# Low parts of the down-projection weights: an adding DMA in place of a VectorE subtraction

## The chip, the cores and the metric

The kernel runs on one core of a Trainium2 chip. The core has TensorE (matrix products, PE in the profile), VectorE (DVE), ScalarE (ACT), GpSimd (POOL) and SyncE (SP, which issues nearly all DMAs), an on-chip memory of 128 partitions (SBUF), accumulators for TensorE (PSUM) and 16 DMA engines. The metric is the device time of one execution in microseconds (us), the median of several runs.

## The reference

One layer of a streaming encoder, in float32, for a group of 512 tokens and a group of 8 x 16 tokens, which share all weights (640 tokens in all, D = 1024):

```python
x = x + 0.5 * swiglu(rms_norm(x, p['norm_ffn1']), p['w_ffn1_up'], p['w_ffn1_down'])
m, st = mixer(rms_norm(x, p['norm_mix']), p, lb, cache, win_rows)
x = x + m
x = x + 0.5 * swiglu(rms_norm(x, p['norm_ffn2']), p['w_ffn2_up'], p['w_ffn2_down'])

def swiglu(h, w_up, w_down):
    gate, val = jnp.split(h @ w_up, 2, axis=-1)
    return (jax.nn.silu(gate) * val) @ w_down
```

The mixer holds a windowed attention, a gated linear recurrence and a convolution with a scan; the change does not touch it. It touches the last product of each SwiGLU, the down-projection: `w_down` has 2816 rows and 1024 columns.

## The kernel before, in words

Activations stand transposed, with features on the partitions and the 640 tokens along a row, in two halves of 320. TensorE multiplies in fp32r, a rounded form of float32. To keep float32's accuracy each operand is split in a high part (the value rounded to fp32r) and a low part (the value minus the high part), and a product is the sum of three: high x high, high x low, low x high.

An item of `proj` is one 128-column strip of a weight matrix with `nk` blocks of 128 rows. Its weight is loaded into a buffer `wr` (three of them), rounded into `wh` (two of them) by ScalarE or VectorE, and the difference goes into `wl` (two of them) by a VectorE subtraction. Then TensorE runs six matmuls for each block: two halves of `wh` with the activations' high parts, two of `wh` with their low parts, two of `wl` with their high parts, into two accumulators `pp`. An item with 8 blocks has 48 matmuls, one with 6 blocks 36.

A feed-forward part (`ffn`) runs in three stages over rows of the hidden size: rows 0 to 5 (in blocks of 128), 6 to 13 and 14 to 21. In the first stage the hidden values come from plain `proj` items with 8 blocks each, in the others from `pair`, which computes seven products of combinations instead of eight, and whose own splits (lines 799 to 829) run on VectorE and ScalarE and use one `wl`, one `wh` and one `wr` as well. At the end of each stage stand eight down-projection items, `proj(wd, ...)` (line 879), one per block of output columns, whose result VectorE adds to the residual (L373). So there are 2 x 3 stages with 8 down-projection items each: 16 items with 6 blocks and 32 with 8. The third stage of the first part also stores the residual and prepares the next norm, that of the second part writes the output.

The order of the work is made before the program is built: `Sched` plays all operations through with costs (a VectorE pass 0.066 us + 1.042 ns an element, a DMA by its bytes) and gives each engine its list; an engine works its list strictly in that order and waits at each instruction for what it needs. `lag` sets how many items ahead an operation is due: 4 for a weight load, 2 for the rounding, 1.5 for the subtraction. A buffer is given to the next item when its last reader is through: `wr` after the rounding and the subtraction, `wl` after the item's last matmul.

Of the kernel before, what the change touches and what calls it, by code (L numbers as in the profile page):

```python
# [8 lines left out]
F32 = mybir.dt.float32  # L9
# [3 lines left out]
AF = mybir.ActivationFunctionType  # L13
ALU = mybir.AluOpType
AX = mybir.AxisListType

P = 128
# [28 lines left out]
class View:  # L46
# [14 lines left out]
    def r(self, pattern, **sizes):  # L61
        return self._then(lambda a: a.rearrange(pattern, **sizes))
# [273 lines left out]
def trunk_kernel(ctx: ExitStack, tc: tile.TileContext, A: dict, O: list):  # L336
    nc = tc.nc
    S = Sched()
# [7 lines left out]
    def dve(n, f, aps=0):  # L346
        return ("DVE", 0.066 + 1.042e-3 * n + 0.063 * aps, f)

    def act(n, f, aps=0, src=None):
        return ("ACT", 0.1 + 0.833e-3 * n + 0.093 * aps - (0.049 if src is not None and src.in_psum else 0.0), f)  # L350
# [7 lines left out]
    def tt(out, a, b, op, only=None):  # L358
        alts = [dve(out.n, lambda: nc.vector.tensor_tensor(out(), a(), b(), op=op))]  # L359
        return S.op(pick(alts, only), [a, b], [out])  # L360
# [11 lines left out]
    def stt(out, a, s, b, op0, op1):  # L372
        return S.op([dve(out.n, lambda: nc.vector.scalar_tensor_tensor(out(), a(), ap_of(s), b(), op0=op0, op1=op1),  # L373
                         isinstance(s, View))], [a, s, b], [out])

    def fn(out, a, func, scale=1.0, bias=0.0, accum=None):
        aps = isinstance(scale, View) + isinstance(bias, View) + (accum is not None)
        kw = {}

        def f():  # L380
            if accum is not None:
                kw["accum_out"] = accum()
            nc.scalar.activation(out(), a(), func, bias=ap_of(bias), scale=ap_of(scale), **kw)  # L383

        return S.op([act(out.n, f, aps, a)], [a, scale, bias], [out] + ([accum] if accum is not None else []),
                    func=None if func in ANY_TABLE else func)
# [15 lines left out]
    def dma(out, a, lag=None):  # L402
        v = out if isinstance(out, View) else a
        return S.op([("SP", 0.47, lambda: nc.sync.dma_start(ap_of(out), ap_of(a)))], [a], [out],  # L404
                    dma=v.n * 4 * v.proto.shape[0], lag=lag)

    def mm(calls):

        def cost(o, l, m):
            if l.proto.dtype == F32R:  # L410
                return max(0.144, m.n * 0.4583e-3)
            w = o.proto.shape[0]
            return {32: 0.021 + 0.415e-3 * m.n, 64: max(0.112, 0.93e-3 * m.n)}.get(w, max(0.216, 0.011 + m.n / 600.0))

        dur = sum(cost(*c[:3]) for c in calls)

        def f():
            for o, l, m, s, e in calls:
                nc.tensor.matmul(o(), l(), m(), start=s, stop=e)  # L419

        return S.op([("PE", dur, f)], [x for c in calls for x in c[1:3]], [c[0] for c in calls])
# [116 lines left out]
    def xk(m):  # L538
        return X.v.r("p (k t) -> p k t", k=KD)[:, m, :].at(m)
# [112 lines left out]
    def halves(v, ps):  # L652

        return [(hv(v)[:, i, :], p[:, :HT]) for i, p in enumerate(ps)]
# [53 lines left out]
        stt(r.v, u.v, 1.5, r.v, ALU.add, ALU.mult)  # L708


    def proj(w, r0, nk, c0, R):

        S.item += 1
        wr, wh, wl = S.buf("wr"), S.buf("wh"), S.buf("wl")
        r, h, l = (b[:, :nk, :] for b in (wr, wh, wl))
        dma(r, w[r0:r0 + nk * P, c0:c0 + P].rearrange("(k p) f -> p k f", p=P), lag=4)
        S.op([act(nk * P, lambda: nc.scalar.copy(h(), r())), dve(nk * P * 0.5, lambda: nc.vector.tensor_copy(h(), r()))], [r], [h], lag=2)  # L717
        S.op([dve(nk * P, lambda: nc.vector.tensor_tensor(l(), r(), h().bitcast(F32), op=ALU.subtract))], [r, h], [l], lag=1.5)  # L718
        ps = [S.buf("pp") for _ in range(2)]
        for k in range(nk):  # L720
            mm([(ps[i][:, :HT], a[:, k, :], R[:, o + k, i * HT:(i + 1) * HT].at(o + k), k == 0 and j == 0, k == nk - 1 and j == 2)
                for j, (a, o) in enumerate(((wh, 0), (wh, 8), (wl, 0))) for i in range(2)])
        return ps

    def scaled(tag, ps, late=False):

        b = S.buf(tag)
        for i, (o, p) in enumerate(halves(b.v, ps)):
            if late:
                cp(o, p, only=("ACT", "DVE"))  # L730
            else:
                tt(o, p, hv(RS.v)[:, i, :], ALU.mult)
        if late:
            tt(b.v, b.v, RS.v, ALU.mult)
        return b

    def parts(R, k, v):
        cp(R[:, k, :].at(k), v, only=("ACT",))
        tt(R[:, 8 + k, :].at(8 + k), v, R[:, k, :].at(k).cast(F32), ALU.subtract)
# [118 lines left out]
    def ffn(wu, wd, norm, R, H, sfx, done, aside=()):  # L858
        ops = None
        for f0, nf in ((0, 6), (6, 8), (14, 8)):  # L860
            for f in range(nf):
                for at, job in aside:
                    if at == f0 + f:
                        job()
                if f0:
                    g, u = pair(wu, f0 + f, ops, sfx)
                else:
                    late = not sfx and f < 2
                    g = scaled("fA" + sfx, proj(wu, 0, KD, f * P, R), late)
                    fn(g.v, g.v, AF.Silu)  # L870
                    u = scaled("fB" + sfx, proj(wu, 0, KD, FF + f * P, R), late)
                tt(u.v, g.v, u.v, ALU.mult)
                parts(H, f, u.v)
                if f0 + f == 2:
                    ops, rest = combos(norm, R, sfx)
            if f0 == 0:
                rest()
            for m in range(KD):
                ps = proj(wd, f0 * P, nf, m * P, H)
                for o, p in halves(xk(m), ps):  # L880
                    stt(o, p, 0.5, o, ALU.mult, ALU.add)
                if f0 == 14:
                    done(m)
# [8 lines left out]
    def spill(m):  # L892
        nm.add(m)
        dma(XD[m].at(m), xk(m))

    ffn(A["w_ffn1_up"][0], A["w_ffn1_down"][0], G1, RA, RB, "", spill)
    lru_params()
    nm.rstd()
# [495 lines left out]
    for m in range(KD):  # L1394
        ps = proj(A["w_out"][0], 0, KD, m * P, RA)
# [8 lines left out]
    def finish(m):  # L1404
# [6 lines left out]
        dma(O[1][:, m * P:(m + 1) * P], y[:, TP:T])  # L1411

    ffn(A["w_ffn2_up"][0], A["w_ffn2_down"][0], G2, RB, RA, "2", finish)

    with tc.manual_schedule():
# [33 lines left out]
```

## Time and profile before

| | |
|---|---|
| median of 3 runs | 1941.85 us (1940.84 to 1941.99) |
| profiled execution | 1942.22 us, span 1940.5 us |
| TensorE busy | 1907.8 us, 98% of the span |
| VectorE busy | 1359.5 us, 70% |
| ScalarE busy | 743.8 us, 38% |
| GpSimd busy | 25.3 us, 1% |
| DMA | 156.87 MB, mean 81 GB/s; the packets of the one large queue took 27.6% of 16 engines' span |

The span goes from the first to the last instruction; the profiled execution's own time has 1.7 us around it. In the profile L404 is the line that issues a DMA, L419 that of a matmul, L717 and L718 the rounding and the subtraction of `proj`, L800 and L803 those of `pair`; L359, L365, L373, L383 and L389 are helpers that many places share. An entry such as `wl<-wr,wh` names output and inputs. The down-projection stages run from about 121 to 163, 258 to 314, 412 to 471, 1580 to 1622, 1720 to 1776 and 1875 to 1935 us.

### The profile page before, as it was taken

The page shows a single profiled execution, that of the slowest core. Times are in us where ns is not written, and L with a number is a line of the kernel's source. Part 1 is how long each engine was busy: PE and PEld are TensorE (multiplying, and loading weights), DVE is VectorE, ACT ScalarE, POOL GpSimd, SP SyncE. Part 2 cuts the span into 40 slices and gives each one's busy share as a digit, 9 for nine tenths or more (in the row PEclk, how much of TensorE's full clock was granted, in tenths as well). Part 3 has the DMA queues.
Part 4 walks back from the last instruction along what each step waited for, and adds up shares of the span by engine and source line. Part 5 has one row for each costly group of instructions (what it writes and reads, how often), then busy time and mean ns, then how long its engine had stood idle before and what let it go on. Part 6 is the DMA issues. An engine that isn't in the chain of part 4 may idle for free.

```text
span 1940.5 us, 35075 instructions
## 1 busy us (share of the span) xinstructions
PE 1907.8 (98%) x14702; PEld 1862.7 (96%) x14702; DVE 1359.5 (70%) x2531; ACT 743.8 (38%) x1278; POOL 25.3 (1%) x58
## 2 busy tenths in 40 slices
PE   6999999999999999999999999999999999999999
PEld 5999999999999999989999999999999999999998
DVE  4957947866778783778547787886566867956963
ACT  4324513422478840887102343434212213412420
POOL 0000000000000000000000000000000000000000
PEclk9999999999999999999999999999999999999999
DMA  4223332234322212212322232222422223222322
GB/s 128 81 68 88 88 87 73 81 91 133 90 66 56 63 53 73 72 53 80 88 77 68 84 89 74 81 83 68 135 77 73 70 76 98 80 84 77 87 73 70
DMA packets 304440, 156.87 MB, mean 81 GB/s; under 512 B 22645, under 2 KB 301782, under 8 KB 304282
## 3 DMA queue, kind: packets, MB, share of 16 engines
q1 hardware_dynamic: 304282, 154.63, 27.6%
q8 instruction: 115, 1.88, 0.4%
q14 instruction: 43, 0.35, 0.1%
HBM read 143.32 MB, written 10.63 MB: 79 GB/s over the span
## 4 chain that ended last, share of the span: by engine, by line
PE 93%; DVE 3%; ACT 2%; SPq 1%; DMA 1%; issue 0%; DVEq 0%; ACTq 0%
PE pp L419 84%; PE me L419 4%; PE ml L419 3%; PE ml L427 1%; SPq L404 1%; PE me L427 1%; ACT L383 1%; DVE AR L373 1%; ACT AR L383 1%; DMA SK<-in_attn_sinks_dram 1%; DVE AR L359 1%; DVE wl L718 0%; DVE AR L1188 0%; DVE RB L359 0%; DVE wh L717 0%
## 5 line engine op out<-in xcount | busy, mean ns | idle before, releaser
L419 PE MATMUL pp<-RA,wh 128*128 128x320 f32 x4288 | 837.1, 315 | 4.2 <-DVE AR L359 3.9
L419 PEld LDWEIGHTS pp<-RA,wh 128*128 128x128 f32 x4288 | 674.8, 189 | 15.3 <-issue 7.6
L419 PE MATMUL pp<-RA,wl 128*128 128x320 f32 x2144 | 500.7, 310 | 1.1 <-DVE wl L718 1.1
L419 PE MATMUL pp<-RB,wh 128*128 128x320 f32 x2112 | 404.9, 309 | 1.4 <-DVE AR L359 0.9
L419 PEld LDWEIGHTS pp<-RA,wl 128*128 128x128 f32 x2144 | 362.6, 189 | 1.9 <-DVE wl L718 1.9
L419 PEld LDWEIGHTS pp<-RB,wh 128*128 128x128 f32 x2112 | 333.9, 188 | 2.2 <-DVE AR L359 1.4
L717 DVE CAST wh<-wr 128x1024 fp32r<-128x1024 f32 (+1 forms) x141 | 96.1, 681 | 265.6 <-PE pp L419 265.2
L419 PE MATMUL pp<-RB,wl 128*128 128x320 f32 x1056 | 250.8, 309 | 0.0
L718 DVE TENSOR_TENSOR wl<-wr,wh 128x1024 fp32r<-128x1024 f32 (+1 forms) x188 | 224.4, 1194 | 1.1 <-ACT wh L717 1.0
L419 PEld LDWEIGHTS pp<-RB,wl 128*128 128x128 f32 x1056 | 179.2, 188 | 0.0
L359 DVE TENSOR_TENSOR AR<-AR 128x640 f32<-128x640 f32 (+10 forms) x271 | 143.5, 534 | 27.1 <-ACT AR L383 20.6
L803 ACT CAST RW<-AR 128x512 fp32r<-128x512 f32 x160 | 98.3, 621 | 163.5 <-PE pp L419 109.5
L383 ACT ACTIVATE AR<-AR 128x640 f32<-128x640 f32 (+3 forms) x180 | 110.4, 614 | 85.0 <-DVE AR L359 76.9
L383 ACT ACT_TABLE_LOAD x99 | 127.0, 1283 | 11.5 <-DVE AR L359 9.4
L359 DVE TENSOR_TENSOR AR<-pp,AR 128x320 f32<-128x320 f32 x240 | 113.6, 485 | 22.3 <-PE pp L419 20.2
L419 PE MATMUL pp<-RX,RW 128*128 128x320 f32 x768 | 123.2, 309 | 0.0
L419 PEld LDWEIGHTS pp<-RX,RW 128*128 128x128 f32 x768 | 115.2, 188 | 0.0
L800 DVE TENSOR_TENSOR RW<-AR,RW 128x512 fp32r<-128x512 f32 x160 | 108.8, 685 | 1.0
L717 ACT CAST wh<-wr 128x1024 fp32r<-128x1024 f32 (+1 forms) x47 | 48.4, 1031 | 127.3 <-PE pp L419 127.3
L389 ACT COPY AR<-me 128x128 f32<-128x128 f32 (+3 forms) x73 | 26.2, 375 | 126.0 <-PE me L427 100.0
L373 DVE SCALAR_TENSOR_TENSOR AR<-pp,AR 128x320 f32<-128x320 f32 x96 | 45.9, 485 | 29.9 <-PE pp L419 29.9
L803 ACT CAST wh<-wr 128x1024 fp32r<-128x1024 f32 x32 | 33.6, 1051 | 77.1 <-PE pp L419 77.1
(184 smaller groups left out, 1930.5 us busy)
## 6 DMA issues: line engine op xcount, KB each, us to landing
wr<-in_w_in_dram SPq DMA_DIRECT2D x84, 512.0 KB
wr<-in_w_ffn_up_dram SPq DMA_DIRECT2D x56, 512.0 KB
AR<-in_w_ffn_up_dram SPq DMA_DIRECT2D x32, 512.0 KB
wr<-in_w_ffn_down_dram SPq DMA_DIRECT2D x32, 512.0 KB
wr<-in_w_ffn_down_dram SPq DMA_DIRECT2D x16, 384.0 KB
wr<-in_w_attn_o_dram SPq DMA_DIRECT2D x8, 512.0 KB
AR<-in_state_hgrn_dram SPq DMA_DIRECT2D x8, 512.0 KB
wr<-in_w_lru_o_dram SPq DMA_DIRECT2D x8, 512.0 KB
```

The lines of the kernel that those rows point to most:

```text
L359: alts = [dve(out.n, lambda: nc.vector.tensor_tensor(out(), a(), b(), op=op))]
L373: return S.op([dve(out.n, lambda: nc.vector.scalar_tensor_tensor(out(), a(), ap_of(s), b(), op0=op0, op1=op1), isinstance(s, View))], [a, ...
L383: nc.scalar.activation(out(), a(), func, bias=ap_of(bias), scale=ap_of(scale), **kw)
L389: alts = [act(out.n, lambda: nc.scalar.copy(out(), a()), 0, a), dve(out.n * (1.0 if a.in_psum else 0.5), lambda: nc.vector.tensor_copy(out ...
L404: return S.op([("SP", 0.47, lambda: nc.sync.dma_start(ap_of(out), ap_of(a)))], [a], [out], dma=v.n * 4 * v.proto.shape[0], lag=lag)
L419: nc.tensor.matmul(o(), l(), m(), start=s, stop=e)
L427: nc.tensor.transpose(o(), i(), d())
L717: S.op([act(nk * P, lambda: nc.scalar.copy(h(), r())), dve(nk * P * 0.5, lambda: nc.vector.tensor_copy(h(), r()))], [r], [h], lag=2)
L718: S.op([dve(nk * P, lambda: nc.vector.tensor_tensor(l(), r(), h().bitcast(F32), op=ALU.subtract))], [r, h], [l], lag=1.5)
L800: S.op([dve(out.n, lambda: nc.vector.tensor_tensor(out(), a(), b(), op=op))], [a, b], [out], lag=lag)
L803: S.op([act(out.n, lambda: nc.scalar.copy(out(), a()))], [a], [out], lag=lag)
```

## The change

For the 48 down-projection items the low part is made in two steps. ScalarE writes the negative of the weight into `wl`, in fp32r, so that `wl` holds the negative of the rounded weight. Then GpSimd issues a DMA from `wr` to `wl` (SBUF to SBUF) that adds what it brings to what stands there: weight minus rounded weight. The DMA has `lag=1.9`, the negation `lag=2`. All other items keep the subtraction.

```diff
-    def proj(w, r0, nk, c0, R):
+    def proj(w, r0, nk, c0, R, by_dma=False):
...
-        S.op([dve(nk * P, lambda: nc.vector.tensor_tensor(l(), r(), h().bitcast(F32), op=ALU.subtract))], [r, h], [l], lag=1.5)
+        if by_dma:
+            S.op([act(nk * P, lambda: nc.scalar.activation(l(), r(), AF.Copy, scale=-1.0))], [r], [l], lag=2)
+            S.op([("POOL", 1.0, lambda: nc.gpsimd.dma_start(l(), r(), accum_op=ALU.add))], [r, l], [l], dma=nk * P * P * 4, lag=1.9)
+        else:
+            S.op([dve(nk * P, lambda: nc.vector.tensor_tensor(l(), r(), h().bitcast(F32), op=ALU.subtract))], [r, h], [l], lag=1.5)
...
             for m in range(KD):
-                ps = proj(wd, f0 * P, nf, m * P, H)
+                ps = proj(wd, f0 * P, nf, m * P, H, True)
```

VectorE's list in the first down-projection stage, the difference (768 elements a partition are 6 blocks; the number behind a name is its buffer):

```order
 L717 CAST wh_82<-wr_81 128x768
 L373 SCALAR_TENSOR_TENSOR AR<-pp_86,AR 128x320
-L718 TENSOR_TENSOR wl_84<-wr_81,wh_82 128x768
 L373 SCALAR_TENSOR_TENSOR AR<-pp_87,AR 128x320
 L717 CAST wh_83<-wr_79 128x768
 L373 SCALAR_TENSOR_TENSOR AR<-pp_88,AR 128x320
-L718 TENSOR_TENSOR wl_85<-wr_79,wh_83 128x768
 L373 SCALAR_TENSOR_TENSOR AR<-pp_89,AR 128x320
```

The casts and the additions to the residual stay in place, the subtractions between them are gone.

ScalarE's list at the same place (L807 is the rounding of `pair`, L803 before):

```order
 L717 CAST wh_83<-wr_80 128x768
-L389 CAST RB<-AR 128x640
-L803 CAST RW_1256<-AR 128x512 x4
+L719 ACTIVATE wl_85<-wr_80 128x768
+L389 CAST RB<-AR 128x640
+L719 ACTIVATE wl_84<-wr_81 128x768
+L719 ACTIVATE wl_85<-wr_79 128x768
+L719 ACTIVATE wl_84<-wr_80 128x768
+L719 ACTIVATE wl_85<-wr_81 128x768
+L719 ACTIVATE wl_84<-wr_79 128x768
+L807 CAST RW_1274<-AR 128x512 x2
```

The negations of successive items stand one behind the other, and each waits there until its `wl` is free; the roundings of the next pair come behind them.

GpSimd's list, from the second to the third stage of the first feed-forward part:

```order
+L720 DMA wl_84<-wr_79 128x1024
+L720 DMA wl_85<-wr_81 128x1024
+L720 DMA wl_84<-wr_81 128x1024
+L720 DMA wl_85<-wr_80 128x1024
+L399 MEMSET RW_3635 128x1024 x4
+L720 DMA wl_84<-wr_81 128x1024
+L720 DMA wl_85<-wr_79 128x1024
+L720 DMA wl_84<-wr_80 128x1024
```

GpSimd's list had no DMA; it now has 48, and four fills for the attention stand between the second and the third of the third stage. On TensorE the list is the same but for a few places: in the first stage of each part one block of six matmuls no longer stands inside another item, and in the last stage the output's transposes move by one block of six.

## The prediction

> **What bounds it now.** I read the page's share of busy time first, then the 40 slices, the chain of waits, and then single stages.
>
> ```profile
> span 1940.5 us, 35075 instructions
> PE 1907.8 (98%) x14702; PEld 1862.7 (96%) x14702; DVE 1359.5 (70%) x2531; ACT 743.8 (38%) x1278; POOL 25.3 (1%) x58
> PE 93%; DVE 3%; ACT 2%; SPq 1%; DMA 1%; issue 0%; DVEq 0%; ACTq 0%
> ...
> 120.00:163.00 43.00, 43.00 (x297) 42.91 (x297) 24.87 (x43) 6.21 (x9) 0.00 (x0) 1.00 0.34 99
> 163.00:477.00 314.00, 314.00 (x2143) 314.00 (x2142) 228.41 (x374) 109.96 (x174) 4.21 (x6) 1.00 0.31 90
> 1548.00:1930.00 382.00, 382.00 (x2616) 381.95 (x2615) 262.84 (x430) 113.03 (x185) 0.00 (x0) 1.00 0.28 81
> ```
>
> TensorE is busy 98% of the span and makes 93% of the chain. The last three rows (window, length, then PE, PEld, DVE, ACT, POOL, clock, DMA share, GB/s) cover all six down-projection stages but the last one's end, and there TensorE has no idle time at all, while VectorE is busy 58% (24.87 of 43), 73% and 69%. So the subtractions that go away are not what anything waits for. TensorE's waits by releaser, over the whole run:
>
> ```profile
> PE me L427 <- DMA RX<-in_x_prompt_dram: 11.2, 2, 11.0
> PE ml L427 <- DMA SK<-in_attn_sinks_dram: 6.1, 1, 6.1
> PE pp L419 <- DVE AR L359: 4.8, 3, 3.6
> PE me L419 <- ACT NH L389: 2.4, 1, 2.4
> PE pp L419 <- DVE wl L718: 1.1, 2, 0.6
> PE me L419 <- DVE NL L359: 0.8, 1, 0.8
> ```
>
> Waits that VectorE ended with a named line sum to some 7 us, 1.1 of it on a low part of a weight. Little can be gained.
>
> **What is removed and added.** There are 48 down-projection items: 16 with 6 blocks of rows (768 columns a partition, 384 KB) and 32 with 8 (1024 columns, 512 KB).
>
> ```profile
> L718 DVE TENSOR_TENSOR wl<-wr,wh x188: 948/1216/1228, 17.2 to 1920.4; 128x1024 fp32r<-128x1024 f32 x172, 128x768 fp32r<-128x768 f32 x16
> L717 ACT CAST wh<-wr x47: 827/1049/1061, 16.2 to 1855.2; 128x1024 fp32r<-128x1024 f32 x43, 128x768 fp32r<-128x768 f32 x4
> L717 DVE CAST wh<-wr x141: 559/694/811, 19.2 to 1919.4; 128x1024 fp32r<-128x1024 f32 x129, 128x768 fp32r<-128x768 f32 x12
> ```
>
> VectorE loses 16 x 0.95 + 32 x 1.22 = 54 us of work. By the shape of ScalarE's rounding pass, ScalarE gains 16 x 0.83 + 32 x 1.05 = 47 us. VectorE's saving is off the path; ScalarE is busy 14 to 35% of these windows (6.21 of 43, 109.96 of 314), so neither total counts. Its cover would be gone where ScalarE owed something to TensorE at once; then a pass would cost its 0.83 to 1.05 us.
>
> What counts is the time from "the low-part buffer is free" to "the low part is there". There are two wl buffers, so the buffer of item m is free when item m-2's last matmul has read it, and only item m-1 lies between. TensorE's rhythm, at the border of two 6-block items and over one 8-block item:
>
> ```profile
> 142.62 0.62 PEld L419 LDWEIGHTS pp<-RB,wh 128*128 128x128 f32 x4
> ...
> 147.90 0.62 PEld L419 LDWEIGHTS pp<-RB,wh 128*128 128x128 f32 x4
> 147.95 0.84 ACT L717 CAST wh<-wr 128x768 fp32r<-128x768 f32 x1 [0.15 <-PE pp L419]
> ...
> 148.49 0.34 PEld L419 LDWEIGHTS pp<-RB,wl 128*128 128x128 f32 x2
> 1885.74 7.05 PE pp L419 x48
> ```
>
> A 6-block item takes 147.90 - 142.62 = 5.28 us, an 8-block item 7.05; the low part is first wanted 0.59 us into an item. From release to want are thus 5.87 us and 7.64 us. In it now stand a cast and a subtraction on VectorE (0.56 + 0.95 or 0.69 + 1.22 us) and 4 us or more of slack. Afterwards stand ScalarE's pass (0.84 or 1.05), two handoffs (0.2 together; ScalarE started 0.05 after the border above), and the whole DMA, from issue to visible. Room for that DMA: 5.87 - 0.84 - 0.2 = 4.83 us for 6 blocks, 7.64 - 1.05 - 0.2 = 6.39 us for 8.
>
> If it takes x longer than the room, the item is late by x, and the next is not (its buffer was released before the delay); every second item pays. In the first stage of each FFN up-projection items of the same ring come before, so items 1, 3, 5, 7 pay; in the other four stages the last paired-tile product frees its wl early and items 2, 4, 6 pay. Sum of the change = 2 x 4 x6 + 4 x 3 x8 = 8 x6 + 12 x8.
>
> **The DMA's time.** The trace has no DMA issued by GpSimd and none that adds. Nearest rows: a load of 512 KB issued at 148.17 for which VectorE stood waiting, the windows of a like load alone (last columns: DMA share, GB/s), the fastest stretch of SBUF stores, and SBUF to SBUF copies.
>
> ```profile
> 148.17 0.37 SPq L404 DMA_DIRECT2D AR<-in_w_ffn_up_dram  x1
> 152.14 0.69 DVE L800 TENSOR_TENSOR AR<-AR 128x512 f32<-128x512 f32 x1 [1.08 <-DMA AR<-in_w_ffn_up_dram]
> 139.70:140.20 0.50, 0.50 (x5) 0.50 (x5) 0.00 (x0) 0.00 (x0) 0.00 (x0) 1.00 0.00 0
> 140.20:140.70 0.50, 0.50 (x5) 0.50 (x4) 0.00 (x0) 0.00 (x0) 0.00 (x0) 1.00 0.22 55
> 140.70:141.20 0.50, 0.50 (x6) 0.50 (x5) 0.00 (x0) 0.00 (x0) 0.00 (x0) 1.00 0.78 231
> 141.20:141.70 0.50, 0.50 (x5) 0.50 (x4) 0.00 (x0) 0.00 (x0) 0.00 (x0) 1.00 0.99 297
> 141.70:142.20 0.50, 0.50 (x6) 0.50 (x5) 0.00 (x0) 0.00 (x0) 0.00 (x0) 1.00 1.14 344
> 142.20:142.70 0.50, 0.50 (x5) 0.50 (x5) 0.03 (x1) 0.00 (x0) 0.00 (x0) 1.00 0.41 121
> 424.60:425.10 0.50, 0.50 (x5) 0.50 (x4) 0.00 (x0) 0.00 (x0) 0.00 (x0) 1.00 1.11 428
> 498.00:498.50 0.50, 0.50 (x4) 0.31 (x3) 0.00 (x0) 0.50 (x2) 0.00 (x0) 1.00 1.00 215
> ```
>
> Issue to use of 512 KB is 152.14 - 148.17 = 3.97 us. Its packets fill between 1.77 us (0.5 x the sum of the shares) and 2.5 us (five windows), so 1.5 to 2.2 us are fixed; I take 1.9. For the data: the add must read the weight and what stands in the buffer, two streams. At 428 GB/s one stream of 512 KB takes 1.22 us, two take 2.45; at the copies' 215 GB/s, 2.44 and 4.88. The copies are nearer in kind but moved between halves of the partitions (64 each); here all 128 partitions take part, as in the stores. I take two streams at 428 GB/s, which is also one at 215. So the DMA takes 1.9 + 2.45 = 4.35 us (8 blocks) and 1.9 + 1.84 = 3.74 us (6), and x6 = x8 = 0. Spare are 2.0 and 1.1 us, for whatever GpSimd's issue costs more than SP's 0.37 and for a weight load running beside it.
>
> Low end: one stream at 428, 1.5 + 1.22 = 2.7 us; zero too. High end: 2.2 + 4.88 + 1.77 for a whole load beside + 0.66, if the issue costs like the 1025 ns below and not 367: 9.5 us, and 2.2 + 3.66 + 1.33 + 0.66 = 7.9 us for 6 blocks. Then x8 = x6 = 3.1 and the sum is 20 x 3.1 = 62 us.
>
> ```profile
> L404 SPq DMA_DIRECT2D RX<-in_x_prompt_dram x4: 597/1025/2946, 1.5 to 13.0; - x4
> L404 SPq DMA_DIRECT2D wr<-in_w_ffn_down_dram x48: 367/368/612, 89.6 to 1898.9; - x48
> 412.28 3.64 POOL L399 MEMSET RW<- 128x1024 f32 x4 [410.97 <-PE pp L419]
> ```
>
> [...]
>
> The queues. On ScalarE the new pass waits for TensorE, and behind it stand the rounding passes of the next pairs (L803) and, in the first FFN's third stage, the copies and squares of the residual; all are wanted an item later or more. The tight place is item 7 of a first stage, where ScalarE does the cast of wh ahead of the negation: room 4.83 - 0.84 = 3.99, still over 3.74. On POOL the four fills of 3.64 us stand between the third stage's second and third accumulation; they are free to run at 412.28, about when that stage's first item starts, and the third accumulation cannot start before that item ends 7 us later, so they hide. On SP the load of item m+3 now waits for the accumulation of item m instead of a VectorE pass: at the latest at item m's start plus 0.6, which leaves two items, 10.6 us or more, for 3.97. Data volume: 48 accumulations of 1.84 to 2.45 us against stages of 42 to 56 us with a DMA share of 0.3 to 0.4: no bound.
>
> Sum: 0. Against the profiled execution (1942.22 us, span 1940.5) that is 1942; the median of the runs is 1941.85. Small overruns only add, so I write 1943. A difference of 0.2%, 3.9 us, is about what this kernel's runs can tell.
>
> **Rivals.** (1) The accumulation takes the place of the pass it removes: slower. Place: the wl ring; it decides once the DMA exceeds 4.83 or 6.39 us. With two streams at the copies' rate, 1.9 + 4.88 = 6.78 and 1.9 + 3.66 = 5.56 us: x8 = 0.39, x6 = 0.73, sum 5.8 + 4.7 = 10.5, time 1953; at the high end 2004. For it: the spare room for 6 blocks is only 1.1 us, and GpSimd's issue is unmeasured. Against it: the load that follows an accumulation is issued when that one lands, so its packets are mostly over when the next one's begin.
>
> (2) VectorE holds GpSimd up while it casts: the DMA of each item starts later by one cast, at most 0.56 (6 blocks) and 0.69 us (8). Within the spare room that is nothing; on top of rival 1 it adds 8 x 0.56 + 12 x 0.69 = 12.8: 1966. Against it: wh and wl are freed by the same matmul, so the cast (0.56) ends before ScalarE's pass (0.84) does and GpSimd only then has its turn. [...]
>
> (3) Faster, because VectorE's relief shortens its other answers to TensorE: at most the some 7 us of such waits, 1935; but they lie outside the windows without idle time, so hardly beside a down-projection.
>
> That the change does not do what it says is out: GpSimd's queue holds 48 such DMAs and 48 subtractions are gone.
>
> **Chances.** No change 0.47; rival 1 0.38; rival 2 0.08; rival 3 0.04; a ScalarE or SP queue upset by the shifted order, slower by a few us, 0.03. So faster 0.04, within 0.2% 0.47, slower 0.49. The likeliest case's own range is 1939 to 1946; the range to hold 8 in 10 goes up to 1988, which leaves out the top of rivals 1 and 2 and the gain.
>
> **What would show it.** Right: TensorE's idle in the six stages stays near 0, and no wait of TensorE on DMA wl. Rival 1: rows "PE pp <- DMA wl" in every second item, and an issue-to-use time above 4.83 or 6.39 us. Rival 2: GpSimd's DMA begins only at the end of a VectorE cast. Wrong altogether: TensorE waits while the accumulation is on time, or a stage without down-projection changes.

## The result, and the profile after

The changed kernel takes 1954.07 us (median of 4 runs, 1952.9 to 1954.68). The kernel before, run beside it and counted with its earlier runs, has 1941.92 us (4 runs, 1940.84 to 1944.06). The ratio is 1.0061, with a 95% interval of 1.0045 to 1.0077: slower by 12.1 us or 0.6%. That lies within the range, but not at the forecast of no change; it is what the first rival said, which had priced it at 10.5 us (1953). The chances had slower (0.49) level with no change (0.47): the range holds because of the rivals, while the sum of 0 does not.

The profiled execution took 1952.9 us with a span of 1951.1, so the trace holds 1951.1 - 1940.5 = 10.6 us of the 12.1. First the head of its page: the span, busy time by engine, and from the lists of DMA queues and of DMA issues the rows of the new DMA (count, KB each, median us from issue to landing).

```profile
span 1951.1 us, 35217 instructions
PE 1909.9 (98%) x14702; PEld 1861.1 (95%) x14702; DVE 1313.9 (67%) x2485; ACT 785.9 (40%) x1324; POOL 67.1 (3%) x106
...
q0 software_dynamic: 6912, 23.07, 6.4%
...
q8 instruction: 115, 1.88, 0.4%
...
wl<-wr POOLq DMA_DIRECT2D x32, 512.0 KB, 4.6
wl<-wr POOLq DMA_DIRECT2D x16, 384.0 KB, 4.5
```

The swap of work is near the forecast (54 and 47): VectorE 1359.5 to 1313.9 us (some 46 less), ScalarE 743.8 to 785.9 (some 42 more). GpSimd's busy time, 25.3 to 67.1 us, counts the issuing of its 48 DMAs (41.8 us). TensorE's own work has not grown (1907.8 and 1909.9 us, the same 14702 matmuls); the time went into its waits. By releaser (sum in us, count, longest):

```profile
PEld pp L419 <- DMA wl<-wr: 9.2, 11, 1.7
PE pp L419 <- DMA wl<-wr: 6.3, 9, 1.4
...
PEld pp L419 <- DVE RA L359: 0.6, 1, 0.6
...
PEld pp L419 <- ACT RA L389: 0.5, 1, 0.5
```

PEld (the weight load) and PE (the matmul) tell the same stops twice, so I count the PEld rows: eleven stops on the adding DMA, 9.2 us. The two RA stops (activations, 1.1 us, both in FFN2's first stage) wait for no DMA. They stand in experiment 5 below too, and there, as TensorE's matmuls set beside those of before show, that stage takes 1.0 us longer; experiment 1 has neither the stops nor the microsecond. So some 1.0 of the 12.1 us goes with the order of the lists that have the DMA in them, not with waiting for it. Where the stops lie is seen in the windows of the six down-projection stages, in order of time (window, length, PE, PEld, DVE, ACT, POOL, clock, DMA share, GB/s):

```profile
120.00:165.00 45.00, 42.54 (x287) 41.71 (x287) 18.15 (x34) 10.56 (x15) 5.21 (x6) 1.00 0.63 148
256.00:316.00 60.00, 59.59 (x407) 59.33 (x406) 20.09 (x36) 10.89 (x13) 5.20 (x6) 1.00 0.60 140
410.00:478.00 68.00, 67.10 (x455) 66.33 (x454) 29.97 (x48) 19.27 (x25) 9.73 (x11) 1.00 0.61 155
1575.00:1628.00 53.00, 49.90 (x332) 48.33 (x331) 24.90 (x44) 17.86 (x25) 6.95 (x8) 1.00 0.61 138
1718.00:1782.00 64.00, 64.00 (x439) 64.00 (x438) 26.46 (x47) 14.77 (x20) 6.10 (x7) 1.00 0.61 145
1870.00:1945.00 75.00, 74.96 (x520) 74.65 (x519) 26.14 (x48) 14.28 (x23) 6.08 (x7) 1.00 0.53 125
```

TensorE was busy through all of these stages before. Now the weight load lacks 45.00 - 41.71 = 3.3 us in the first window and 53.00 - 48.33 = 4.7 in the fourth (the 6-block stages), 0.7 and 1.7 in FFN1's two others, and in FFN2's two others 0 and 0.35. The clock is 1.00 throughout, so it is no cause.

How one item loses time, first in FFN1's first stage, from the timeline (start, us; the bracket holds the idle time before and its releaser):

```profile
126.57 0.85 ACT L719 ACTIVATE wl<-wr 128x768 fp32r<-128x768 f32 x1 [4.43 <-PE pp L419]
127.78 0.89 POOL L720 DMA_DIRECT2D wl<-wr  x1 [4.48 <-ACT wl L719]
132.63 0.30 PEld L419 LDWEIGHTS pp<-RB,wl 128*128 128x128 f32 x2 [0.50 <-DMA wl<-wr]
```

The negation ends at 127.42 and GpSimd's row begins 0.36 later. The DMA lands 4.8 us after its issue, at 132.58, and TensorE goes on at 132.63, having stood 0.50 us: the low part was wanted at 132.13. From the issue that is 4.35 us, where the prediction had 4.83. At 8 blocks (VectorE's cast of wh, ScalarE's negation, GpSimd's issue) the issue stands 1.47 us after the start of its negation:

```profile
273.86 0.69 DVE L717 CAST wh<-wr 128x1024 fp32r<-128x1024 f32 x1 [5.55 <-PE pp L419]
274.15 1.06 ACT L719 ACTIVATE wl<-wr 128x1024 fp32r<-128x1024 f32 x1 [5.98 <-PE pp L419]
275.62 0.88 POOL L720 DMA_DIRECT2D wl<-wr  x1 [6.18 <-ACT wl L719]
```

Again 0.41 us pass between the negation's end and GpSimd. The largest stops are another thing. There are two of 1.71 us, at the last item of either FFN's first stage:

```profile
148.37 1.16 ACT L807 CAST RW<-AR 128x512 fp32r<-128x512 f32 x2 [4.61 <-DVE AR L804]
149.44 0.83 ACT L717 CAST wh<-wr 128x768 fp32r<-128x768 f32 x1
150.18 0.84 ACT L719 ACTIVATE wl<-wr 128x768 fp32r<-128x768 f32 x1
...
151.43 0.88 POOL L720 DMA_DIRECT2D wl<-wr  x1 [6.46 <-ACT wl L719]
...
152.34 0.37 SPq L404 DMA_DIRECT2D AR<-in_w_ffn_up_dram  x1
...
156.51 0.30 PEld L419 LDWEIGHTS pp<-RB,wl 128*128 128x128 f32 x2 [1.71 <-DMA wl<-wr]
```

ScalarE has two passes for the next stage's pairs and the cast of wh ahead of the negation in its list. The first of them stood until 148.37 for a VectorE subtraction (L804), and the negation starts at 150.18, right behind the cast.

That is only a part of the stop. TensorE wanted the low part at 156.51 - 1.71 = 154.80, 3.37 us after the issue; a DMA of 3.9 us, which is what one of 6 blocks takes alone (see below), would have been 0.5 us late. This one lands after 5.0 us, its twin in FFN2 after 5.1. By the single packets its first one came at 1.45 us, as alone, but its packets of 3 KB took 376 ns on average (371 in FFN2), where those of the other 14 DMAs of 6 blocks took 253 to 269. These two are the only ones of the 16 behind which SP issues a load less than 3.9 us later (at 152.34, 0.9 us behind); the packets of that load come after theirs.

The third kind is seen in FFN1's third stage. Two adding DMAs, with what SP issued between them, and below them the traffic by queue in 460.3 to 463.1 and in 463.1 to 466.5 (packets, MB, share of 16 engines; q1 holds SP's DMAs, q0 GpSimd's):

```profile
452.27 0.89 POOL L720 DMA_DIRECT2D wl<-wr  x1 [6.18 <-ACT wl L719]
...
459.11 0.37 SPq L404 DMA_DIRECT2D wr<-in_w_in_dram  x1
459.56 0.87 POOL L720 DMA_DIRECT2D wl<-wr  x1 [6.40 <-ACT wl L719]
459.56 0.53 SPq L404 DMA_DIRECT2D x_mid<-AR  x1
...
466.86 0.30 PEld L419 LDWEIGHTS pp<-RB,wl 128*128 128x128 f32 x2 [0.71 <-DMA wl<-wr]
```

```profile
q1 hardware_dynamic: 1091, 0.73, 90.6%
```

```profile
q0 software_dynamic: 143, 0.52, 77.8%
q1 hardware_dynamic: 63, 0.11, 8.2%
```

The first of the two lands at 459.07 (6.8 us after its issue); only that frees wr, and SP issues the next weight load at 459.11. The next adding DMA follows at 459.56, and a store of x_mid at the same time. Until 463.1 the 16 DMA engines moved the load and most of the store, and nothing of the adding DMA. From the single packets, for a few of the 48 (us after the issue; KB are those of SP's queue between the issue and the adding DMA's first packet):

```
issued   blocks  first packet  last packet ends  landed  KB of SP's queue ahead
116.97     6       1.44            3.59            3.9        0
133.05     6       2.14            4.42            4.7      329
144.11     6       2.32            5.02            5.4      404
268.57     8       1.43            4.20            4.5        0
303.78     8       3.24            6.15            6.5      940
452.27     8       3.13            6.49            6.8      718
459.56     8       3.59            6.96            7.3      743
```

Alone, then, an adding DMA takes 3.9 us (6 blocks) or 4.5 us (8) from issue to landing, and fits its room. Behind SP's traffic it takes up to 7.3.

### The profile page after: what moved, and what is told of

It reads as the page before. It is cut to its first block, busy times and chain, and to the rows that moved or that the text cites. A ratio compares the mean times of both kernels' runs of the same rounds, so it can differ in the third digit from the quotient of the medians.

```text
span 1951.1 us, 35217 instructions
## 1 busy us (share of the span) xinstructions
PE 1909.9 (98%) x14702; PEld 1861.1 (95%) x14702; DVE 1313.9 (67%) x2485; ACT 785.9 (40%) x1324; POOL 67.1 (3%) x106
## 3 DMA queue, kind: packets, MB, share of 16 engines
q8 instruction: 115, 1.88, 0.4%
## 4 chain that ended last, share of the span: by engine, by line
PE 88%; issue 4%; DVE 3%; DMA 2%; ACT 2%; SPq 1%; POOL 0%; POOLq 0%; DVEq 0%; ACTq 0%
PE pp L419 79%; PE me L419 4%; PE ml L419 3%; DMA wl<-wr 1%; PE ml L427 1%; SPq L404 1%; PE me L427 1%; ACT L383 1%; DVE AR L373 1%; DMA SK<-in_attn_sinks_dram 1%; ACT AR L383 1%; DVE AR L359 1%; POOL wl L720 0%; DVE wl L722 0%; DVE AR L1192 0%
## 5 line engine op out<-in xcount | busy, mean ns | idle before, releaser
L722 DVE TENSOR_TENSOR wl<-wr,wh 128x1024 fp32r<-128x1024 f32 x140 | 170.3, 1216 | 1.2 <-ACT wh L717 1.0
L807 ACT CAST RW<-AR 128x512 fp32r<-128x512 f32 x160 | 98.5, 621 | 128.9 <-PE pp L419 108.1
L719 ACT ACTIVATE wl<-wr 128x1024 fp32r<-128x1024 f32 (+1 forms) x48 | 47.5, 990 | 162.3 <-PE pp L419 162.3
L804 DVE TENSOR_TENSOR RW<-AR,RW 128x512 fp32r<-128x512 f32 x160 | 109.2, 686 | 2.0 <-ACT RW L807 0.3
L720 POOL DMA_DIRECT2D wl<-wr x48 | 41.8, 871 | 999.5 <-ACT wl L719 965.1
```

The lines of the kernel that those rows point to most:

```text
L719: S.op([act(nk * P, lambda: nc.scalar.activation(l(), r(), AF.Copy, scale=-1.0))], [r], [l], lag=2)
L720: S.op([("POOL", 1.0, lambda: nc.gpsimd.dma_start(l(), r(), accum_op=ALU.add))], [r, l], [l], dma=nk * P * P * 4, lag=1.9)
L804: S.op([dve(out.n, lambda: nc.vector.tensor_tensor(out(), a(), b(), op=op))], [a, b], [out], lag=lag)
L807: S.op([act(out.n, lambda: nc.scalar.copy(out(), a()))], [a], [out], lag=lag)
```

## The experiments

Each diff is against the changed kernel. Times are medians; each ratio is to the kernel before on the same chip, with its 95% interval. Runs 1 to 4 shared one set of runs of the kernel before (median 1942.13 us), 5 to 8 another (1941.79), 9 to 11 a third (1942.17).

**1. Without the DMA.** The ring's whole cost, or is part of it ScalarE's new pass and the shifted lists?

```diff
-            S.op([("POOL", 1.0, lambda: nc.gpsimd.dma_start(l(), r(), accum_op=ALU.add))], [r, l], [l], dma=nk * P * P * 4, lag=1.9)
```

> The negation by ScalarE stays, the adding DMA is left out (the low part then holds the negated rounded weight, so the products are wrong). Theory A (the DMA's way from the free wl buffer to the landed low part is longer than TensorE's cover): no wait of TensorE on DMA wl, about 1942 us, as before the change. Rival (the 48 passes on ScalarE and the shifted lists cost the time themselves): TensorE still waits 9 us or so in the six stages, and the time stays above 1948.

Measured: 1942.3 us, ratio 1.0002 (0.9993 to 1.0012). The only stops left on a wl are those of ordinary items, as before:

```profile
PEld pp L419 <- DVE wl L721: 1.9, 3, 0.8
```

So the 48 passes on ScalarE and the lists as they shift in this run cost nothing, and the 48 subtractions that VectorE no longer does gain nothing. The cost needs the DMA: its waits, and to some 1.0 us the lists made with it.

**2 and 3. Only the 6-block items, only the 8-block items by DMA.**

```diff
-                ps = proj(wd, f0 * P, nf, m * P, H, True)
+                ps = proj(wd, f0 * P, nf, m * P, H, nf == 6)
```

> The DMA only in the 16 items with 6 blocks, whose item lasts 5.28 us; the 32 others keep the subtraction. Theory A, from the changed kernel's trace: TensorE's waits in the two first stages, 3.2 + 3.6 on DMA wl and 1.0 on other parts there, so 7 to 8 us, 1949 to 1950. Rival (each DMA costs the same): 12.1 x 16 / 48 = 4.0 us, 1946.

> The DMA only in the 32 items with 8 blocks, whose item lasts 7.04 us. Theory A: 0.7 + 1.7 us of waits as in the changed kernel's trace, about 1944.5, with the waits late in a stage only. Rival (each DMA costs the same): 12.1 x 32 / 48 = 8.1 us, 1950.

Measured, with `nf == 6`: 1951.87 us, ratio 1.0053 (1.0038 to 1.0068). With `nf == 8`: 1943.73 us, ratio 1.0011 (1.0002 to 1.0021). TensorE's stops on the DMA, 6 blocks first:

```profile
PEld pp L419 <- DMA wl<-wr: 7.2, 7, 1.8
```

```profile
PEld pp L419 <- DMA wl<-wr: 2.2, 3, 1.2
```

16 of the 48 DMAs cost 9.7 us (the two RA stops among them), the other 32 only 1.6; together 11.3 of the 12.1. The 6-block items are the tight ones, since their room is an item of 5.28 us and not 7.05. The cost of the first was somewhat above what was expected (7 to 8), that of the second below.

**4. Negation and DMA in two halves.** Each half of the blocks gets its own negation, its own DMA and its own wait. The first half of a buffer comes free half an item earlier, and the second half is wanted half an item later; the data are the same.

```diff
+            for i, (b0, b1) in enumerate(((0, nk // 2), (nk // 2, nk))):
+                lb, rb = wl[:, b0:b1, :].at(i), r[:, b0:b1, :]
...
-            mm([(ps[i][:, :HT], a[:, k, :], R[:, o + k, i * HT:(i + 1) * HT].at(o + k), k == 0 and j == 0, k == nk - 1 and j == 2)
+            mm([(ps[i][:, :HT], a[:, k, :].at(k * 2 // nk if by_dma and a is wl else None), R[:, o + k, i * HT:(i + 1) * HT].at(o + k), k == 0 and j == 0, k == nk - 1 and j == 2)
```

> Negation and adding DMA in two halves of the blocks, each half of the wl buffer with its own wait, so that the first half can start when the earlier item's first half of blocks is read, and the second half is wanted half an item later. Theory A: room grows by 2.6 us (6 blocks) and 3.5 us (8 blocks), waits on DMA wl fall below 2 us in all, 1942 to 1944. Rival (GpSimd's issue or the DMA's fixed part is the price, 0.87 us each on POOL): twice as many DMAs, no gain or worse, 1954 to 1965.

Measured: 1942.66 us, ratio 1.0003 (0.9994 to 1.0013), with twice as many DMAs:

```profile
PEld pp L419 <- DMA wl<-wr: 0.3, 1, 0.3
...
L722 POOL DMA_DIRECT2D wl<-wr x96: 859/869/1217, 105.6 to 1919.7; - x96
```

The cost is gone, though 96 DMAs with a median landing of 3.6 us do the work of 48. So it was a matter of room in the ring, not of the DMA's volume or of GpSimd's time. The kernel is not faster than before either: with TensorE busy there is nothing to gain. It is the best form of the change, and it beats neither kernel by anything that can be measured.

**5. A plain copy in place of the adding one.** The low part then holds the whole weight.

```diff
-            S.op([("POOL", 1.0, lambda: nc.gpsimd.dma_start(l(), r(), accum_op=ALU.add))], [r, l], [l], dma=nk * P * P * 4, lag=1.9)
+            S.op([("POOL", 1.0, lambda: nc.gpsimd.dma_start(l(), r()))], [r, l], [l], dma=nk * P * P * 4, lag=1.9)
```

> The same DMA as a plain copy, without the addition (the low part then holds the whole weight, so the products are wrong). If the second stream that the addition reads sets the data time: packets of a 512 KB DMA take 1.3 to 1.6 us instead of 2.77, issue to landing falls from 4.5 to about 3.2 us, TensorE's waits on DMA wl from 9 to 2 us or less, 1943 to 1946. If the path from SBUF to SBUF or the change of type sets it: 2.7 us and 4.5 us stay, and so does 1954.

Measured: 1943.22 us, ratio 1.0008 (0.9999 to 1.0017); no stop on the DMA at all, but the two RA stops. The rows of the DMA, of the changed kernel and of the copy (ns of one issue, shortest, median, longest; then us from issue to landing):

```profile
L720 POOL DMA_DIRECT2D wl<-wr x48: 859/868/1010, 107.6 to 1931.3; - x48
...
DMA to landing us min/median/max: 3.9/4.6/7.3
```

```profile
L720 POOL DMA_DIRECT2D wl<-wr x48: 530/530/670, 107.6 to 1921.1; - x48
...
DMA to landing us min/median/max: 2.6/2.9/5.0
```

The addition costs 0.34 us more at the issue. By the single packets, 512 KB take 2.77 us with it and 1.46 without (339 and 175 ns for 4096 bytes): 2.77 / 1.46 = 1.9 times as long.

**6. A second cast of wh on VectorE behind the negation.** Does VectorE hold GpSimd up?

```diff
+            S.op([dve(nk * P * 0.5, lambda: nc.vector.tensor_copy(h(), r()))], [r, l], [h], lag=1.95)
```

> VectorE rounds wh of each of the 48 items a second time, started by the end of the negation, so at the moment of GpSimd's issue. Theory A: GpSimd's issue stays at 0.87 us, the time within 2 us of the changed kernel's 1954. [...]

Measured: 1953.19 us, ratio 1.0058 (1.0041 to 1.0075), as without it. But the run does not decide. A pair of rows from FFN1's second stage shows why:

```profile
275.88 0.68 DVE L720 CAST wh<-wr 128x1024 fp32r<-128x1024 f32 x1
276.63 0.88 POOL L721 DMA_DIRECT2D wl<-wr  x1 [6.18 <-ACT wl L719]
```

The cast ends at 276.56, before GpSimd begins. It was over too early, and experiment 11 repeats the question with three casts.

**7. Twice the bytes in the plan.** The planner is told that the DMA moves twice as much; the list order changes, the work does not.

```diff
-..., dma=nk * P * P * 4, lag=1.9)
+..., dma=nk * P * P * 8, lag=1.9)
```

> Only the bytes that the planner counts for the adding DMA are doubled, so that its modelled time (5.2 and 6.3 us) is nearer to the measured 3.9 to 7.3; the work is the same, the lists differ. Theory A: the waits of 1.7 us at the last item of the two first stages, where ScalarE's list has the next pair's roundings ahead of the negation, may go, 2 to 3 us in all, the other waits stay: 1951 to 1953. Rival (the lists' order is the whole cause): back to 1943.

Measured: 1952.27 us (1949.48 to 1954.38), ratio 1.0051 (1.0036 to 1.0066).

```profile
PEld pp L419 <- DMA wl<-wr: 6.3, 10, 1.9
```

The stops shrink from 9.2 to 6.3 us in the profiled execution, which is the fastest of this kernel's runs (1949.48); the last item of the two first stages stops for 1.45 and 0.83 us instead of 1.71 twice. The interval takes in the changed kernel's own ratio. A truer cost in the planner does not mend it.

**8. Half of the load.** For the 48 items only half of the blocks are loaded; the other half of wr keeps what it held.

```diff
-        dma(r, w[r0:r0 + nk * P, c0:c0 + P].rearrange("(k p) f -> p k f", p=P), lag=4)
+        nl = nk // 2 if by_dma else nk
+        dma(wr[:, :nl, :], w[r0:r0 + nl * P, c0:c0 + P].rearrange("(k p) f -> p k f", p=P), lag=4)
```

> The weight load of each of the 48 items brings only the first half of the blocks (the rest of the buffer keeps what was there, so the products are wrong), which halves its packets' time from 2.1 to about 1.0 us. Theory A with the collision (a late accumulation releases the load that then stands ahead of the next accumulation in the DMA engines): the landings of 5.4 to 7.3 us fall by about 1 us, the waits on DMA wl from 9.2 to 5 to 7 us, 1949 to 1952. If the loads have no part in it: landings and 1954 stay.

Measured: 1948.73 us, ratio 1.0037 (1.0023 to 1.005).

```profile
PEld pp L419 <- DMA wl<-wr: 6.2, 8, 1.9
```

Landing times in us, item by item, of the changed kernel and of this one:

```
FFN1, first stage, changed kernel   4.1 3.9 3.9 4.8 4.7 4.3 5.4 5.0
FFN1, first stage, half of load     4.6 3.9 3.9 3.9 3.9 3.9 4.6 5.0
FFN1, third stage, changed kernel   4.5 4.6 4.8 4.9 4.9 6.1 6.8 7.3
FFN1, third stage, half of load     4.5 4.6 4.8 4.7 4.8 5.9 6.3 6.7
```

In the first stage the middle items land after 3.9 us, as if alone: the load was what delayed them. The two stops at the last items stay (1.85 and 1.88 us), and so do their landings (5.0 and 5.1): the load issued behind these DMAs belongs to the next pairs, and this edit leaves it whole. Without those, the changed kernel's stops are 9.2 - 2 x 1.71 = 5.8 us, and here 6.2 - 3.7 = 2.5. In the third stage the loads beside the last items belong to the next part of the layer (in_w_in above), which this edit leaves whole, and there the late landings remain. So the loads that are halved make more than half of the other stops: 5.8 - 2.5 = 3.3 us of stops, and 1953.6 - 1948.7 = 4.9 us of time, if 1.0061 is applied to this set's 1941.79 (a difference of two medians with intervals of 0.3%, so a rough size).

**9. The cast of wh only on VectorE** for these items, so that it cannot stand ahead of the negation on ScalarE.

```diff
-        S.op([act(nk * P, lambda: nc.scalar.copy(h(), r())), dve(nk * P * 0.5, lambda: nc.vector.tensor_copy(h(), r()))], [r], [h], lag=2)
+        S.op(pick([act(nk * P, lambda: nc.scalar.copy(h(), r())), dve(nk * P * 0.5, lambda: nc.vector.tensor_copy(h(), r()))], ("DVE",) if by_dma else None), [r], [h], lag=2)
```

> The cast of wh of the 48 items only on VectorE, so that at the last item of the two first stages ScalarE has no cast of 0.83 us ahead of the negation (the roundings of the next pair stay ahead of it). Theory A with ScalarE's order as the cause of those two waits of 1.7 us: each falls to about 0.9 us, the others stay, 1952 to 1953. If these waits come from a DMA that lands late for another reason: 1.7 us each stay and so does 1954.

Measured: 1951.57 us, ratio 1.0051 (1.0034 to 1.0068).

```profile
PEld pp L419 <- DMA wl<-wr: 9.9, 13, 1.6
```

A miss. The two stops at the last items were to fall to 0.9 us; they are 1.24 and 1.56. In FFN1 the negation came some 0.8 us earlier within the item, but its DMA then took 5.9 us to land instead of 5.0: its first packet came at 2.42 us, behind 414 KB of SP's queue. In FFN2 the landing took 5.5 instead of 5.1. The order on ScalarE makes these items later, but taking one pass away only moves the DMA into other traffic.

**10. The negation on VectorE.** Is ScalarE, or a pass of 1.06 us instead of some 0.69, the cause?

```diff
-            S.op([act(nk * P, lambda: nc.scalar.activation(l(), r(), AF.Copy, scale=-1.0))], [r], [l], lag=2)
+            S.op([dve(nk * P * 0.5, lambda: nc.vector.tensor_scalar(l(), r(), -1.0, None, op0=ALU.mult))], [r], [l], lag=2)
```

> The negation by VectorE (as a multiplication by -1) in place of ScalarE; the DMA stays. Theory A: the pass is as short as VectorE's cast, 0.56 or 0.69 us in place of 0.84 or 1.05, but stands behind the cast in the same list, so it ends 0.2 to 0.3 us later than before; the waits of the last items fall as the pair's roundings on ScalarE are no longer ahead: waits of 6 to 10 us in all, 1949 to 1955. Rival (ScalarE's use is the cost): back to 1943.

Measured: 1954.09 us, ratio 1.006 (1.0045 to 1.0075).

```profile
PEld pp L419 <- DMA wl<-wr: 11.2, 11, 1.8
```

```profile
274.84 0.69 DVE L717 CAST wh<-wr 128x1024 fp32r<-128x1024 f32 x1 [4.95 <-PE pp L419]
275.45 0.69 DVE L719 TENSOR_SCALAR wl<-wr 128x1024 fp32r<-128x1024 f32 x1
...
276.54 0.88 POOL L720 DMA_DIRECT2D wl<-wr  x1 [6.18 <-DVE AR L373]
```

The pass is shorter, 0.69 us, and the time is the same: on VectorE it stands behind the cast of wh. From that cast's start to GpSimd's row are 276.54 - 274.84 = 1.70 us here and 275.62 - 273.86 = 1.76 in the changed kernel. So the DMA starts no sooner in the item, and the choice of engine is not the cause.

**11. Three casts on VectorE while GpSimd issues.**

```diff
+            for _ in range(3):
+                S.op([dve(nk * P * 0.5, lambda: nc.vector.tensor_copy(h(), r()))], [r, l], [h], lag=1.95)
```

> As with the second cast, but three more casts of wh by VectorE from the end of the negation on, so that VectorE is casting while GpSimd's issue of 0.87 us runs and not just before it. Theory A: GpSimd's issue stays at 0.87 us and landings at 3.9 and 4.5 us where nothing collides; the time within 3 us of the changed kernel's 1954 (VectorE has more to do, and its casts may come late for the next item). [...]

Measured: 1955.68 us, ratio 1.0072 (1.0057 to 1.0087). Now they overlap:

```profile
275.82 1.19 POOL L722 DMA_DIRECT2D wl<-wr  x1 [5.87 <-ACT wl L719]
276.07 1.57 DVE L721 CAST wh<-wr 128x1024 fp32r<-128x1024 f32 x2
...
L722 POOL DMA_DIRECT2D wl<-wr x48: 859/1063/1200, 107.0 to 1932.9; - x48
```

The issue grows from 0.87 to 1.19 us under two casts, and an 8-block landing that is not held up by SP's traffic from 4.5 to 4.8. So VectorE does hold GpSimd up here, by about 0.3 us for a DMA and not by a whole cast of 0.69, let alone two. The casts grow too, 1.57 us for two where one takes 0.69. What makes them slow each other was not shown. In the changed kernel, issues of 859 to 1010 ns (median 868) leave next to no room for the effect.

## Why the prediction was right or wrong, point by point

**TensorE bounds, VectorE's relief gains nothing: right.** Experiment 1 does all the rest of the change and has 1.0002. With it rival 3 (faster, 1935) falls.

**The DMA alone: right, 3.74 and 4.35 us forecast, 3.9 and 4.5 measured.** Its parts: 1.43 us to the first packet and some 0.3 behind the last, together 1.7 where 1.9 stood, and packets of 2.16 and 2.77 us where 1.84 and 2.45 stood. Of the two choices (two streams, and the stores' rate rather than the copies') the first fits experiment 5 (packets 1.9 times as long with the addition), and the second lay near: 2 x 512 KB in 2.77 us are 379 GB/s, between the 428 taken and the 215 set aside. Rival 1's price of the DMA, 5.56 and 6.78 us, was too high.

**The room: the term that was mis-sized.** "two handoffs (0.2 together...)" measured some 0.7. GpSimd begins 0.36 to 0.41 us after the negation ends. And the row from which the other handoff was read, a cast that starts 0.05 us after the item's border, waited for wh, which the item's last two matmuls no longer read; wl is what they read, so its buffer is free some 0.3 us later. The room is 4.35 us for 6 blocks, not 4.83, and by the same steps 7.64 - 0.3 - 1.06 - 0.4 = 5.9 for 8 blocks, not 6.39. Against 3.9 and 4.5 that leaves 0.45 and 1.4 us instead of 1.1 and 2.0. By itself this would still have been no change.

**"The load that follows an accumulation is issued when that one lands, so its packets are mostly over when the next one's begin": wrong, and the step that failed.** It was written as a reason against rival 1. It holds only while the DMA lands well before it is wanted. When it lands at the last moment, the load is issued about 0.5 to 1 us ahead of the next adding DMA (459.11 and 459.56 above), whose first packet then comes after 3.59 us instead of 1.43. That one is late too, releases wr late, and meets the next load in the same way: in FFN1's third stage the last three land after 6.1, 6.8 and 7.3 us. With a margin of 0.45 us one such meeting suffices. Experiment 8 makes the load smaller and the middle landings return to 3.9 us; experiment 4 enlarges the margin and the whole cost goes. I had put "a weight load running beside it" into the spare room and into the high end of the range, but not into the value taken.

**"room 4.83 - 0.84 = 3.99, still over 3.74": wrong.** The place, item 7 of a first stage, was right. Ahead of the negation stood not the cast of wh alone but two passes of the next pairs too (1.16 us), "all ... wanted an item later or more"; that they are not urgent does not keep them from standing in front. These two items hold 3.4 of the 9.2 us. By the rows above the late negation makes 0.5 us of each stop, and the longer landing, with a load issued right behind the DMA, the other 1.2. Experiment 9 took one pass away and got 2.8 instead of 3.4, its DMAs landing later still.

**The pattern "every second item pays": wrong.** In the first stage of FFN1 items 3, 6 and 7 pay, in the second only the last, in the third the last three; FFN2's second and third stages pay nothing. A constant overrun would make every second item late. What came is a small margin that single meetings use up, mostly towards the end of a stage. So rival 1 came true by its place (the wl ring) and nearly by its sum (10.5 against 12.1), but not by its mechanism: its slow DMA of 5.56 and 6.78 us in every item is not there, and its split (5.8 for 6 blocks, 4.7 for 8) is measured as 9.7 and 1.6.

**Rival 2: not here.** By experiment 11 the effect is 0.3 us for a DMA if the casts overlap it. A delay by a whole cast, 0.56 or 0.69 us, as that rival priced it (12.8 us in all), no run shows. In the changed kernel the casts are over before the issue (at 274.55 us against 275.62 in the rows above), as the prediction argued.

**The queues on POOL and the DMA volume: right.** The fills fell into the time that the list left for them, no stop names them, and experiment 4 moves the same bytes in 96 DMAs at no cost.

What stays open: of the 12.1 us, 9.2 are seen as stops on the DMA and some 1.0 as RA stops in the profiled execution, which was the fastest of the four runs; the further 1.5 us of the median are in no trace. No run isolates the RA stops: that they come from the lists is read from their being there in experiment 5 and missing in experiment 1. In the two 8-block stages that pay, the DMA with which the late landings begin (issued at 296.74 and 445.24, landing after 5.5 and 6.1 us) also had a 16 KB packet of q8, the queue that the page names instruction, beside it; whether the chain would have begun without that is not known. Why FFN2's third stage pays nothing and FFN1's does was not tried; the loads of the next part and the stores of x_mid, which stand beside the last items in FFN1 only, fit it.

## What to carry to other kernels

When a step in a double-buffered ring is replaced by a DMA, compare the room from the buffer's release to its first use with the whole of the DMA's latency, and read the release and every handoff from rows of that very buffer: here 0.5 us of handoffs, and 0.16 of the DMA, took the margin from 1.1 to 0.45 us. Then ask what the landing releases: if the DMA also holds the buffer that a load waits for, a late landing sends that load in front of the next such DMA, and lateness feeds itself (landings of 6.1, 6.8 and 7.3 us in a row here); splitting the buffer in halves with waits of their own took the whole cost away (ratio 1.0003). And relief of an engine that nothing waits for is worth nothing, however many microseconds of work it is (46 here).

## What the runs showed of the hardware that was not expected

- The adding DMA cost more at the issue as well: 868 ns of GpSimd (median) against 530 for a plain copy of the same tile in experiment 5.
- Some adding DMAs began late, behind packets that SP's queue already had under way. With 743 KB of them (issue at 459.56) the first packet came 3.59 us after the issue, when nearly all of those had gone, and with none ahead after 1.43 us. What holds the DMA back was not tested.
- Adding DMAs with a load issued right behind them took longer. Packets of 3 KB took 376 and 371 ns on average in the two DMAs with a load 0.9 us behind, and 253 to 269 in the other 14; experiments 2, 7, 8 and 10 show 363 to 374 wherever a load follows by 0.9 to 1.0 us. In experiment 5 the plain copy's packets took 180 and 178 ns at the same two places and 139 to 150 elsewhere. The records show the load's packets only behind the DMA's; what slows these was not tested.
- Some adding DMAs were late with no load beside them. The one issued at 1724.38 landed after 6.4 us; its first packet came at 1.46 us, but its last ended at 5.8 instead of 4.2, and in that time one engine carried a 16 KB packet of q8 (instruction). This is read from packet records alone, and no run isolates it.
